# Memory transposes written ahead of the last head pair's q and k, and new tiles for the memory's low parts and two outputs

## The chip, the cores and the metric

One core of a Trainium2 chip runs the whole program, one execution at a time. The metric is the device time of one execution in microseconds. Before the change it is 1638.81 us (median of 3 runs, 1638.03 to 1639.77).

## The reference

A trunk of two layers over 512 tokens of width 1024, all in f32. Each layer has three sublayers, and each of these adds its normalised result to the running state:

```python
h = h + rms_norm(mixer(rms_norm(h, mix_pre_g[i])), mix_post_g[i])
y = memory_cross_attention(rms_norm(h, mem_pre_g[i]), rms_norm(mem, mem_kv_g[i]),
                           x_wq[i], x_wkv[i], x_wo[i])
h = h + rms_norm(y, mem_post_g[i])
h = h + rms_norm(swiglu_ffn(rms_norm(h, ffn_pre_g[i]), w_gate_up[i], w_down[i]), ffn_post_g[i])
```

The mixer of layer 0 is dilated attention: 16 heads of 64, three patterns of window and stride whose softmaxes are merged. The mixer of layer 1 is differential attention: 8 heads, each with two softmaxes, `(p1 - lam * p2) @ v`, and an RMS norm of each head's output. Cross attention has 4 heads of 256 over 256 memory tokens: the queries come from the state, keys and values from the normalised memory. What matters below is that the memory's keys and values depend on the memory and on weights alone, and so can be computed at any time before the cross attention.

## The kernel before

**Number format.** Every large product is made of three fp32r products: each operand is split into a high part (a rounded copy) and a low part (what is left), and hi*hi, hi*lo and lo*hi are added in PSUM. A split is one ScalarE copy and one VectorE subtract: L229/L230 for activations, L269/L270 for a weight page of 128x1024, L320/L321 behind a transpose.

**Storage.** R[0] to R[21] are tiles of 128x2x512, high part and low part side by side. A tile has many tenants in turn. PSUM has eight banks: banks 0 and 1 (in the mixers) collect projections, 2, 4 and 5 take attention scores, 3 takes probability times value ("pv"), 6 and 7 take transposes alternately. f0 to f3 hold softmax rows, f8 and f9 hold outputs, wh0 to wh2 and wl0 to wl2 hold split weights. A spare weight also goes into R tiles when those are free; the lists of "spares" (L1358 for the cross attention) say which tile and from which mark on.

**The mixer.** Heads are worked on in 8 pairs. `ORDER` (L895) says in which order the projections are written: `v` a quarter of the values, `k`, `q` or `p` (both) for one pair, `m` the loading and normalising of the memory's two halves into the tiles named g0 and m7 (m7 lies in R[7]). Attention of a pair is: scores (L683, L684), softmax, transposes of the probability tiles (L316), pv (L757 in layer 0; L780 to L782 in layer 1), output. In layer 1 the output of a head goes through a mean square by matmul (L791), a VectorE transpose of blocks (L793), an inverse root on GpSimd (L797), the transpose back (L798) and the scaling L802, after which PSUM bank 3 is free for the next pv. Outputs are split into R[p], pair p.

**The memory.** `mem_T` transposes the two halves, four blocks of 128x512 in all (four PE transposes, one ScalarE copy and one VectorE subtract each): high parts into R[8] and R[9], low parts into R[16] and R[17]. `x_kv(0)` then makes keys (L344 to L346) and values (L953 to L955) of the first cross head. Both stand in `early`, between the mixer and its output projection `close` (w_out, L396 to L398). The first line of `early` waited for pair 6's scores and a mark of the weights; `pair_ready` (L737) let the attention of pair 7 begin only when `mem_T` had been written.

**What sets the order.** `drive` (L182) writes two streams into each other, "dense" (projections) and "att" (attention), by their estimated cost and by conditions that a stream yields. The program so written then goes through a scheduler which orders each engine's queue by the data dependencies and the position in the program; everything of the attention stream is written at a priority 200 positions ahead. On the chip each queue runs from front to back.

**Behind the last scores.** The FFN's first weights are folded sums: SyncE loads (L1158, L1161, L1164, L1166), GpSimd DMAs which add onto the loaded data (L1159, L1162), and VectorE additions (L1175). The tile "fold0" lies where pair 7's last operands of the scores (page1 in layer 0, qz in layer 1) lay, and so its first load comes after the last score.

## Time and profile before

| | |
|---|---|
| median of 3 runs | 1638.81 us |
| the profiled execution | 1638.14 us |
| its span, first to last instruction | 1636.4 us |
| TensorE busy | 1580.5 us, 97% of the span |
| VectorE, ScalarE, GpSimd busy | 67%, 48%, 22% |
| mean granted TensorE clock | 0.993 |

The span leaves 1.74 us of the execution's own time around it. In the rows below, a bracket such as `[0.34 <-DVE r L321]` says that the engine stood idle for 0.34 us before the instruction and which instruction ended that wait. Buffer numbers are left out in the trace (r for any R tile). In the rows of the order they stand, with a running number behind an underscore (r8_75 is R[8]).

### The profile page before, as it was taken

How to read it: one execution, taken by the hardware profiler on the slowest of the kernel's cores; microseconds unless marked ns; L12 is line 12 of the kernel's file. 1: busy time of each engine (PE TensorE's matmuls, PEld its weight loads, DVE VectorE, ACT ScalarE, POOL GpSimd, SP SyncE). 2: the span in 40 equal slices, each digit the busy share in tenths (PEclk: the TensorE clock that was granted, in tenths of full speed). 3: DMA queues.
4: the chain of work that ended last, by engine and by line, in shares of the span. 5: the costliest groups of instructions: out<-in, count | busy, mean ns of one | idle time of the engine just before them, and what ended most of it. 6: DMA issues, size and time to landing. Idle time of an engine off the chain costs nothing.

```text
span 1636.4 us, 25877 instructions
## 1 busy us (share of the span) xinstructions
PE 1580.5 (97%) x10064; PEld 1427.0 (87%) x10064; DVE 1089.3 (67%) x1750; ACT 779.4 (48%) x1349; POOL 365.5 (22%) x356
## 2 busy tenths in 40 slices
PE   6999989999989999999999999889999999999998
PEld 6899878899878999988898888778988899999886
DVE  7778886754557677772378888856555667778332
ACT  5566665543535444452236565634444444445221
POOL 4634420200031111100044654221001321110000
PEclk9999999999999999999999999999999999999999
DMA  5533424343315676633424434343332167774322
GB/s 219 146 91 101 114 73 135 115 131 103 115 50 128 175 181 178 159 107 99 142 91 134 121 101 115 102 145 109 105 113 79 48 179 182 180 180 124 103 91 90
DMA packets 76763, 202.63 MB, mean 124 GB/s; under 512 B 9952, under 2 KB 10208, under 8 KB 76640
## 3 DMA queue, kind: packets, MB, share of 16 engines
q1 hardware_dynamic: 65696, 181.05, 35.7%
q0 software_dynamic: 10944, 19.93, 7.7%
q8 instruction: 79, 1.29, 0.3%
q14 instruction: 44, 0.36, 0.1%
HBM read 178.40 MB, written 2.10 MB: 110 GB/s over the span
## 4 chain that ended last, share of the span: by engine, by line
PE 69%; DVE 12%; DMA 6%; issue 5%; POOL 3%; ACT 3%; SPq 0%; DVEq 0%; POOLq 0%; ACTq 0%
PE bank L396 7%; PE bank L398 7%; PE bank L397 7%; PE bank L1212 6%; PE bank L1214 6%; PE bank L1213 6%; PE bank L344 6%; PE bank L345 6%; PE bank L346 5%; DMA fold<-in_gate_up_s 4%; PE bank L316 3%; PE bank L757 1%; DVE wl L230 1%; DVE wl L270 1%; PE bank L683 1%
## 5 line engine op out<-in xcount | busy, mean ns | idle before, releaser
L270 DVE TENSOR_TENSOR wl<-page,wh 128x1024 fp32r<-128x1024 f32 x128 | 162.6, 1272 | 178.1 <-ACT wh L269 177.5
L269 ACT ACTIVATE wh<-page 128x1024 fp32r<-128x1024 f32 x155 | 163.7, 1057 | 226.2 <-PE bank L398 88.8
L344 PE MATMUL bank<-uh,wh 128*128 128x512 f32 (+1 forms) x576 | 208.3, 363 | 0.5 <-ACT uh L320 0.5
L345 PE MATMUL bank<-ul,wh 128*128 128x512 f32 (+1 forms) x576 | 207.6, 361 | 0.0
L346 PE MATMUL bank<-uh,wl 128*128 128x512 f32 (+1 forms) x576 | 207.1, 360 | 0.0
L229 ACT ACTIVATE wh<-fold 128x1024 fp32r<-128x1024 f32 x114 | 118.5, 1055 | 130.5 <-PE bank L1213 95.9
L304 POOL TENSOR_SCALAR small<-small 128x1 f32<-128x1 f32 x76 | 24.8, 326 | 641.6 <-ACT page L297 641.1
L230 DVE TENSOR_TENSOR wl<-fold,wh 128x1024 fp32r<-128x1024 f32 x114 | 138.4, 1217 | 5.8 <-ACT wh L229 5.7
L396 PE MATMUL bank<-wh,r 128*128 128x512 f32 x336 | 130.9, 394 | 2.9 <-DVE f L802 2.1
L1212 PE MATMUL bank<-r,wh 128*128 128x256 f32 x456 | 129.1, 285 | 2.8 <-DVE f L1261 2.8
L397 PE MATMUL bank<-wl,r 128*128 128x512 f32 x336 | 131.2, 391 | 0.1
L398 PE MATMUL bank<-wh,r 128*128 128x512 f32 x336 | 130.1, 391 | 0.0
L1214 PE MATMUL bank<-uh,wl 128*128 128x256 f32 x456 | 128.8, 283 | 0.0
L1213 PE MATMUL bank<-r,wh 128*128 128x256 f32 x456 | 128.3, 283 | 0.0
L1212 PE MATMUL bank<-uh,wh 128*128 128x256 f32 x456 | 126.0, 283 | 1.9 <-DVE f L1246 1.9
L1214 PE MATMUL bank<-r,wl 128*128 128x256 f32 x456 | 126.4, 283 | 0.0
L1213 PE MATMUL bank<-ul,wh 128*128 128x256 f32 x456 | 126.2, 283 | 0.0
L316 PE MATMUL bank<-ident,f 128*128 128x128 f32 x576 | 95.9, 282 | 30.1 <-DVE f L330 23.6
L344 PEld LDWEIGHTS bank<-uh,wh 128*128 128x128 f32 x576 | 111.2, 194 | 15.8 <-ACT uh L320 0.9
L346 PEld LDWEIGHTS bank<-uh,wl 128*128 128x128 f32 x576 | 111.2, 193 | 14.6 <-issue 0.5
L345 PEld LDWEIGHTS bank<-ul,wh 128*128 128x128 f32 x576 | 111.2, 193 | 14.3 <-DVE ul L321 0.3
L1175 DVE TENSOR_TENSOR fold<-fold 128x512 f32<-128x512 f32 x76 | 52.6, 692 | 99.6 <-DMA fold<-in_gate_up_s 61.5
(227 smaller groups left out, 4473.2 us busy)
## 6 DMA issues: line engine op xcount, KB each, us to landing
fold<-in_gate_up_s SPq DMA_DIRECT2D x114, 256.0 KB, 4.5
page<-in_down SPq DMA_DIRECT2D x44, 512.0 KB, 3.5
fold<-in_gate_up_s SPq DMA_DIRECT2D x38, 512.0 KB, 5.5
fold<-in_gate_up_s POOLq DMA_DIRECT2D x76, 256.0 KB, 5.3
r<-r SPq DMA_DIRECT2D x120, 128.0 KB, 2.3
page<-in_x_wk SPq DMA_DIRECT2D x16, 512.0 KB, 3.5
page<-in_x_wv SPq DMA_DIRECT2D x16, 512.0 KB, 3.5
page<-in_x_wq SPq DMA_DIRECT2D x16, 512.0 KB, 3.5
```

Of the source, the lines that this page charges most:

```text
L230: self.nc.vector.tensor_sub(lo, src, hi.bitcast(F32))
L269: self.nc.scalar.activation(hi, raw, AF.Copy)
L270: (self.nc.gpsimd if eng else self.nc.vector).tensor_tensor(lo, raw, hi.bitcast(F32), ALU.subtract)
L344: nc.tensor.matmul(out, wh[:, k], xh(k)[:, cols], start=k == 0, stop=False)
L345: nc.tensor.matmul(out, wh[:, k], xl(k)[:, cols], start=False, stop=False)
L346: nc.tensor.matmul(out, wl[:, k], xh(k)[:, cols], start=False, stop=k == DK - 1)
L396: nc.tensor.matmul(out, ah[:, ts], hi[:, kk], start=k == 0, stop=False)
L397: nc.tensor.matmul(out, ah[:, ts], lo[:, kk], start=False, stop=False)
L398: nc.tensor.matmul(out, al[:, ts], hi[:, kk], start=False, stop=k == ktiles - 1)
L1212: nc.tensor.matmul(out, wh[:, k], xh[:, k], start=first and k == 0, stop=False, **skip)
L1213: nc.tensor.matmul(out, wh[:, k], xl[:, k], start=False, stop=False, **skip)
L1214: nc.tensor.matmul(out, wl[:, k], xh[:, k], start=False, stop= k == 3, **skip)
```

## The change

`ORDER` gets a step "t" ahead of p7: once the mark ("w", 5) stands, `mem_T` is written there, ahead of the projections of pair 7. The condition on the memory in `pair_ready` goes, and `early` keeps only the gain's load and `x_kv(0)`. `mem_T` takes the four blocks in another order (first half left, second half left, second half right, first half right), and gives R[7] back between the transposes and the split of the third. The low parts go to R[6] and R[7] instead of R[16] and R[17]; the outputs of pairs 6 and 7 go to R[16] and R[17] instead of R[6] and R[7]; the keys and values of cross head 2 go to (16, 17) instead of (6, 7); and the spare weight of the cross attention that uses (16, 17) becomes free with output 5 there instead of with the last keys and values.

```diff
-    def transposes(self, u, hi, lo):
+    def transposes(self, u, hi, lo, between=None):
...
+        if between is not None:
+            between()
         tv = tb.rearrange("p (k t) -> p k t", k=4)
+        hi, lo = (hi(), lo()) if callable(hi) else (hi, lo)
...
             and ("v", p // 2) in m
-            and (p < 7 or "mem" in m)
...
+    def o_tile(self, k):
+        return self.R[k if k < 6 else 10 + k]
...
-                self.split(o32, self.R[p][:, 0], self.R[p][:, 1])
+                self.split(o32, self.o_tile(p)[:, 0], self.o_tile(p)[:, 1])
...
+            if w == "t":
+                yield lambda: ("w", 5) in seen
+                yield from self.mem_T()
+                continue
...
-    ORDER = "v0 k1 p2 v1 p3 p4 v2 p5 m p6 v3 p7"
+    ORDER = "v0 k1 p2 v1 p3 p4 v2 p5 m p6 v3 t p7"
...
-        for b, m in enumerate(self.mem):
+        for b, j in ((0, 0), (1, 0), (1, 1), (0, 1)):
...
+            self.transposes(
+                self.mem[b][:, j * S : (j + 1) * S], hi, lo,
+                (lambda: self.restore(7)) if (b, j) == (1, 1) else None,
+            )
+            yield 0.45
...
-    MEM = ((8, 9), (16, 17))
+    MEM = ((8, 9), (6, 7))
...
-        return [self.R[i] for i in ((21, 18), (12, 13), (6, 7), (21, 18))[hd]]
+        return [self.R[i] for i in ((21, 18), (12, 13), (16, 17), (21, 18))[hd]]
...
-            ((16, 17), has("xkv", 3)),
+            ((16, 17), has("o", 5)),
...
-                yield lambda: ("s", 6) in self.mark and ("w", 5) in self.mark
-                yield from self.mem_T()
                 load(0, "mem_pre_g", i)
```

The lines of the changed kernel that are named below stand 3 to 14 lines further down: L344 becomes L347, L396 L399, L683 L686, L757 L762, L780 L785, L953 L966, L321 L324, L798 L803, L802 L807, L729 L732, L1158 L1171, L1175 L1188.

**TensorE, layer 0, the memory's transposes.** g0 is the first half of the memory, m7 the second, r18 and r19 operands of pair 7's scores, r8 and r9 high parts of the memory, f0 to f3 probability rows. Before:

```order
L316 MATMUL bank7_123<-ident_107,g0_95 128x128 x4
...
L316 MATMUL bank6_122<-ident_107,g0_95 128x128 x4
L683 MATMUL bank5_121<-r19_86,r18_85 128x512
...
L684 MATMUL bank4_120<-r20_87,page1_112 128x512
L953 MATMUL bank0_116<-wh2_91,r8_75 128x256
...
L955 MATMUL bank0_116<-wh2_91,r16_83 128x256
L316 MATMUL bank7_123<-ident_107,m7_1784 128x128 x4
L316 MATMUL bank6_122<-ident_107,m7_1784 128x128 x4
L344 MATMUL bank1_117<-r8_75,wh0_89 128x256
L316 MATMUL bank7_123<-ident_107,f3_100 128x128 x4
```

and now:

```order
L316 MATMUL bank7_123<-ident_107,g0_95 128x128 x4
...
L316 MATMUL bank6_122<-ident_107,m7_1784 128x128 x4
L686 MATMUL bank5_121<-r19_86,r18_85 128x512
...
L687 MATMUL bank4_120<-r20_87,page1_112 128x512
L966 MATMUL bank0_116<-wh2_91,r8_75 128x256
...
L968 MATMUL bank0_116<-wh2_91,r6_459 128x256
L316 MATMUL bank7_123<-ident_107,m7_1784 128x128 x4
L347 MATMUL bank1_117<-r8_75,wh0_89 128x256
L316 MATMUL bank6_122<-ident_107,g0_95 128x128 x4
...
L347 MATMUL bank1_117<-r9_76,wh0_89 128x256
L316 MATMUL bank7_123<-ident_107,f3_100 128x128 x4
L316 MATMUL bank6_122<-ident_107,f0_97 128x128
```

The first transposes keep their place behind three scores of pair 7 (the L684 just ahead of them are not shown), and so pair 7's projections stay ahead of them. The last of the four moves behind the first projection on the memory, and the first transposes of a probability row behind it (f3) now stand 14 matmuls behind the last transposes of the memory, where one stood between.

**VectorE, layer 0, around the first fold addition.** wl2 is the low part of a w_out weight, r13 and r15 transposed probabilities. Before:

```order
L321 TENSOR_TENSOR r15_82<-bank7_123,r14_81 128x4x128
L710 RECIPROCAL small_110<-small_110 128x1
L1175 TENSOR_TENSOR fold0_4147<-fold0_4147 128x512
L321 TENSOR_TENSOR r13_80<-bank6_122,r12_79 128x4x128
L270 TENSOR_TENSOR wl2_94<-page0_111,wh2_91 128x1024
L1175 TENSOR_TENSOR fold0_4147<-fold0_4147 128x512
L230 TENSOR_TENSOR ul_66<-bank0_116,ul_66 128x512
L270 TENSOR_TENSOR wl0_92<-page0_111,wh0_89 128x1024
L321 TENSOR_TENSOR r13_80<-bank7_123,r12_79 128x4x128
```

and now:

```order
L324 TENSOR_TENSOR r15_82<-bank7_123,r14_81 128x4x128
L698 TENSOR_SCALAR f2_99<-f2_99,small_110 128x512
L1188 TENSOR_TENSOR fold0_4147<-fold0_4147 128x512
L270 TENSOR_TENSOR wl2_94<-page0_111,wh2_91 128x1024
L713 RECIPROCAL small_110<-small_110 128x1
L324 TENSOR_TENSOR r13_80<-bank6_122,r12_79 128x4x128
L1188 TENSOR_TENSOR fold0_4147<-fold0_4147 128x512
L230 TENSOR_TENSOR ul_66<-bank0_116,ul_66 128x512
L270 TENSOR_TENSOR wl0_92<-page0_111,wh0_89 128x1024
L324 TENSOR_TENSOR r13_80<-bank7_123,r12_79 128x4x128
```

The split of wl2 has moved ahead of the evacuation of bank 6 into r13; both stand behind the first fold addition, before and now.

**TensorE, layer 0, where the last probability rows are transposed.** wh1, wl1, wh2 and wl2 are w_out weights, r0 to r3 outputs. Before:

```order
L398 MATMUL bank2_118<-wh1_90,r1_68 128x512
L316 MATMUL bank7_123<-ident_107,f1_98 128x128
...
L757 MATMUL bank3_119<-r14_81,r11_78 128x256
L316 MATMUL bank6_122<-ident_107,f2_99 128x128 x4
L757 MATMUL bank3_119<-r15_82,r11_78 128x256
L396 MATMUL bank1_117<-wh2_91,r2_69 128x512
L397 MATMUL bank1_117<-wl2_94,r2_69 128x512
L398 MATMUL bank1_117<-wh2_91,r2_69 128x512
```

and now:

```order
L399 MATMUL bank1_117<-wh2_91,r2_69 128x512
...
L316 MATMUL bank7_123<-ident_107,f1_98 128x128
...
L762 MATMUL bank3_119<-r15_82,r11_78 128x256
L400 MATMUL bank1_117<-wl2_94,r2_69 128x512
L401 MATMUL bank1_117<-wh2_91,r2_69 128x512
L399 MATMUL bank1_117<-wh2_91,r3_70 128x512
L400 MATMUL bank1_117<-wl2_94,r3_70 128x512
L401 MATMUL bank1_117<-wh2_91,r3_70 128x512
L316 MATMUL bank6_122<-ident_107,f2_99 128x128 x4
```

Seven w_out matmuls and one pv matmul have moved ahead of the f2 transposes, and six of them use wh2 or wl2.

**TensorE, layer 1, the first, fourth and last scores of pair 7.** Before:

```order
L316 MATMUL bank6_122<-ident_107,m7_8599 128x128 x4
L683 MATMUL bank5_121<-r19_86,r18_85 128x512
L683 MATMUL bank4_120<-r19_86,r18_85 128x512
...
L344 MATMUL bank1_117<-r8_75,wh1_90 128x256
L683 MATMUL bank5_121<-r19_86,r18_85 128x512
L684 MATMUL bank5_121<-r20_87,qz_7211 128x512
...
L954 MATMUL bank0_116<-wl1_93,r9_76 128x256
L683 MATMUL bank2_118<-r19_86,r18_85 128x512
L684 MATMUL bank2_118<-r20_87,qz_7211 128x512
L955 MATMUL bank0_116<-wh1_90,r17_84 128x256
```

and now:

```order
L316 MATMUL bank6_122<-ident_107,g0_95 128x128 x4
L348 MATMUL bank1_117<-r6_6642,wh1_90 128x256
...
L349 MATMUL bank1_117<-r8_75,wl1_93 128x256
L686 MATMUL bank5_121<-r19_86,r18_85 128x512
...
L348 MATMUL bank1_117<-r7_9023,wh2_91 128x256
L686 MATMUL bank5_121<-r19_86,r18_85 128x512
...
L401 MATMUL bank1_117<-wh2_91,r1_6493 128x512
L686 MATMUL bank2_118<-r19_86,r18_85 128x512
L687 MATMUL bank2_118<-r20_87,qz_7211 128x512
L316 MATMUL bank7_123<-ident_107,f2_99 128x128 x4
```

Eleven projections on the memory now stand ahead of the first scores, the fourth score (the second on bank 5) follows 26 matmuls behind them, and the last score (bank 2) stands behind the whole of x_kv(0) and six w_out matmuls.

**VectorE, layer 1, the end of the attention.** f9 and f8 belong to the output of pair 6, f2 to the last probability rows of pair 7. Before:

```order
L270 TENSOR_TENSOR wl1_93<-page0_6398,wh1_90 128x1024
L1175 TENSOR_TENSOR fold0_10875<-fold0_10875 128x512
L321 TENSOR_TENSOR r15_82<-bank7_123,r14_81 128x4x128
L798 STREAM_TRANSPOSE f9_106<-small_110 128x512
L1175 TENSOR_TENSOR fold0_10875<-fold0_10875 128x512
L729 SCALAR_TENSOR_TENSOR f2_99<-f2_99,small_110,f3_100 128x512
L270 TENSOR_TENSOR r20_87<-page0_6398,r19_86 128x1024
L802 SCALAR_TENSOR_TENSOR f8_105<-bank3_119,gsub_115,f9_106 128x512
```

and now:

```order
L270 TENSOR_TENSOR r20_87<-page0_6398,r19_86 128x1024
L730 TENSOR_TENSOR small_110<-small_110,lam_114 128x1
L324 TENSOR_TENSOR r15_82<-bank7_123,r14_81 128x4x128
L803 STREAM_TRANSPOSE f9_106<-small_110 128x512
L1188 TENSOR_TENSOR fold0_10875<-fold0_10875 128x512
L807 SCALAR_TENSOR_TENSOR f8_105<-bank3_119,gsub_115,f9_106 128x512
L732 SCALAR_TENSOR_TENSOR f2_99<-f2_99,small_110,f3_100 128x512
L1188 TENSOR_TENSOR fold0_10875<-fold0_10875 128x512
```

The fold addition moves behind the transpose L798 (now L803), and the scaling L802 (now L807) moves up to stand right behind it. On SyncE, at the same time, three loads of w_out now stand ahead of the first load of the fold, where one stood, and the copy of ul stands ahead of the fold's third and fourth load.

## Rows read from the trace of the kernel before

**Rows 1.** The profile's page: its first part (busy time) and the first line of its fourth (shares of the chain that ended last).

```profile
PE 1580.5 (97%) x10064; PEld 1427.0 (87%) x10064; DVE 1089.3 (67%) x1750; ACT 779.4 (48%) x1349; POOL 365.5 (22%) x356
...
PE 69%; DVE 12%; DMA 6%; issue 5%; POOL 3%; ACT 3%; SPq 0%; DVEq 0%; POOLq 0%; ACTq 0%
```

**Rows 2.** Busy time by stretch (start and end in us; PE, PEld, DVE, ACT, POOL busy us with counts; granted TensorE clock; DMA share; GB/s), around the end of each mixer.

```profile
230.00:250.00 20.00, 14.83 (x89) 12.94 (x88) 18.13 (x36) 12.97 (x25) 7.08 (x6) 0.91 0.35 103
250.00:270.00 20.00, 19.63 (x150) 18.72 (x150) 13.09 (x29) 14.28 (x26) 3.03 (x3) 1.00 0.52 145
270.00:290.00 20.00, 18.95 (x94) 15.87 (x95) 11.79 (x15) 7.44 (x11) 0.00 (x0) 1.00 0.46 135
1030.00:1050.00 20.00, 15.85 (x93) 13.85 (x92) 15.88 (x31) 12.07 (x24) 6.73 (x5) 0.83 0.37 106
1050.00:1070.00 20.00, 20.00 (x125) 17.73 (x124) 12.41 (x21) 11.33 (x21) 6.43 (x5) 1.00 0.67 199
1070.00:1090.00 20.00, 15.74 (x77) 11.91 (x75) 11.58 (x15) 4.75 (x7) 3.20 (x2) 1.00 0.31 92
```

**Rows 3.** Timeline of TensorE in layer 0 (start, duration, engine, line, operation, tiles, shape, count, idle time before it and what ended it): the memory's transposes and what follows them.

```profile
247.75 0.28 PE L954 MATMUL bank<-wl,r 128*128 128x256 f32 x1
247.87 0.28 PE L955 MATMUL bank<-wh,r 128*128 128x256 f32 x1
247.99 1.05 PE L316 MATMUL bank<-ident,m 128*128 128x128 f32 x8
249.28 0.39 PE L344 MATMUL bank<-r,wh 128*128 128x256 f32 x1 [0.23 <-ACT r L320]
250.00 0.66 PE L316 MATMUL bank<-ident,f 128*128 128x128 f32 x4 [0.34 <-DVE r L321]
```

**Rows 4.** The same view, the end of the attention in layer 0.

```profile
256.00 0.39 PE L684 MATMUL bank<-r,page 128*128 128x512 f32 x1
...
269.04 0.60 PE L757 MATMUL bank<-r,r 128*128 128x256 f32 x3
270.93 0.66 PE L316 MATMUL bank<-ident,f 128*128 128x128 f32 x4 [1.29 <-DVE r L321]
271.34 0.36 PE L757 MATMUL bank<-r,r 128*128 128x256 f32 x1
271.54 0.40 PE L396 MATMUL bank<-wh,r 128*128 128x512 f32 x1
272.06 0.50 PE L397 MATMUL bank<-wl,r 128*128 128x512 f32 x1
```

**Rows 5.** Timeline of VectorE in layer 0, the same time.

```profile
264.33 0.15 DVE L710 RECIPROCAL small<-small 128x1 f32<-128x1 f32 x1
269.58 0.69 DVE L1175 TENSOR_TENSOR fold<-fold 128x512 f32<-128x512 f32 x1 [5.10 <-DMA fold<-in_gate_up_s]
270.19 0.68 DVE L321 TENSOR_TENSOR r<-bank,r 128x512 fp32r<-128x512 f32 x1
270.79 1.21 DVE L270 TENSOR_TENSOR wl<-page,wh 128x1024 fp32r<-128x1024 f32 x1
271.93 0.68 DVE L1175 TENSOR_TENSOR fold<-fold 128x512 f32<-128x512 f32 x1
```

**Rows 6.** Timeline of TensorE in layer 1: the fourth score of pair 7, its last, and two w_out matmuls.

```profile
1044.98 0.50 PE L683 MATMUL bank<-r,r 128*128 128x512 f32 x1 [0.78 <-ACT f L723]
...
1056.61 0.39 PE L683 MATMUL bank<-r,r 128*128 128x512 f32 x1
1056.84 0.39 PE L684 MATMUL bank<-r,qz 128*128 128x512 f32 x1
...
1069.35 0.39 PE L398 MATMUL bank<-wh,r 128*128 128x512 f32 x1
1069.58 0.39 PE L396 MATMUL bank<-wh,r 128*128 128x512 f32 x1
```

**Rows 7.** The same view, the waits at the end of layer 1's attention.

```profile
1074.78 0.39 PE L780 MATMUL bank<-r,r 128*128 128x256 f32 x1 [0.45 <-DVE f L802]
...
1080.90 1.13 PE L791 MATMUL bank<-f,page 128*128 128x512 f32 x2 [0.92 <-ACT f L787]
1082.84 0.50 PE L396 MATMUL bank<-wh,r 128*128 128x512 f32 x1 [0.81 <-DVE f L793]
...
1090.04 0.47 PE L396 MATMUL bank<-wh,r 128*128 128x512 f32 x1 [2.13 <-DVE f L802]
```

**Rows 8.** Timeline of VectorE in layer 1, the same time.

```profile
1059.92 1.23 DVE L270 TENSOR_TENSOR wl<-page,wh 128x1024 fp32r<-128x1024 f32 x1
...
1069.78 0.69 DVE L1175 TENSOR_TENSOR fold<-fold 128x512 f32<-128x512 f32 x1 [1.57 <-DMA fold<-in_gate_up_s]
...
1073.98 0.74 DVE L802 SCALAR_TENSOR_TENSOR f<-bank,gsub,f 128x512 f32<-128x512 f32 x1
```

**Rows 9.** Timeline of SyncE's DMA issues in layer 1.

```profile
1057.27 0.33 SPq L1158 DMA_DIRECT2D fold<-in_gate_up_s  x1
...
1061.18 0.33 SPq L253 DMA_DIRECT2D page<-in_b_out  x1
```

**Rows 10.** Timeline of GpSimd in layer 1, the same time.

```profile
1062.06 0.95 POOL L1159 DMA_DIRECT2D fold<-in_gate_up_s  x1 [23.43 <-PE bank L791]
...
1064.77 2.93 POOL L797 TENSOR_TENSOR small<-small,mhalf 128x16 f32<-128x16 f32 x1
```

**Rows 11.** Timeline of ScalarE in the cross attention of layer 0: the fourth and fifth weights split into spare tiles.

```profile
423.73 1.06 ACT L269 ACTIVATE r<-page 128x1024 fp32r<-128x1024 f32 x1 [1.34 <-DMA page<-in_x_wo]
...
427.16 1.06 ACT L269 ACTIVATE r<-page 128x1024 fp32r<-128x1024 f32 x1 [1.28 <-DMA page<-in_x_wo]
```

More of the change, by code (lines that the diff above doesn't have):

```diff
@@ L802, in rest @@
                 nc.vector.scalar_tensor_tensor(sq, pv, self.gsub, r, ALU.mult, ALU.mult)
-                self.split(sq, self.R[p][:, 0], self.R[p][:, 1])
+                self.split(sq, self.o_tile(p)[:, 0], self.o_tile(p)[:, 1])
                 self.mark["o", p] = self.clock
@@ L910, in mem_T @@
     def mem_T(self):
-        for b, m in enumerate(self.mem):
+        for b, j in ((0, 0), (1, 0), (1, 1), (0, 1)):
             ts = slice(b * P, (b + 1) * P)
-            for j in range(2):
-                hi, lo = [
-                    self.R[self.MEM[s][j]].rearrange("p a (b t) -> p (a b) t", b=2)[:, :, ts]
-                    for s in (0, 1)
-                ]
-                self.transposes(m[:, j * S : (j + 1) * S], hi, lo)
-                yield 0.45
-        self.restore(7)
+            hi, lo = [
+                lambda i=self.MEM[s][j], ts=ts: self.R[i].rearrange(
+                    "p a (b t) -> p (a b) t", b=2
+                )[:, :, ts]
+                for s in (0, 1)
+            ]
+            self.transposes(
[3 more added lines that the diff above has]
+            yield 0.45
         self.mark["mem"] = self.clock
-    MEM = ((8, 9), (16, 17))
+    MEM = ((8, 9), (6, 7))
     def memr(self, s, k):
@@ L1327, in o_act, with x_act @@
         def o_act(k):
+            return self.o_tile(k)[:, 0], self.o_tile(k)[:, 1]
+        def x_act(k):
             return self.R[k][:, 0], self.R[k][:, 1]
@@ L1410, in emit @@
                 self.close(
-                    t["x_wo"][i], DK, o_act, o_ready, get("mem_post_g"), get("ffn_pre_g"),
+                    t["x_wo"][i], DK, x_act, o_ready, get("mem_post_g"), get("ffn_pre_g"),
                     cross_spares,
```

## The prediction, made before the result was known

> **What bounds the kernel.** I read the page first: TensorE is busy 97% of the span, and the chain that ended last lies on it for 69% [rows 1]. So an edit counts by the gaps that it closes or opens on TensorE; time won on another engine counts only where TensorE waits for it. Next the busy time by stretch, to see whether there are gaps where the change works [rows 2]. Those around the memory's transposes have 14.83 and 15.85 us of work in 20, those behind the last scores 19.63, 18.95, 20.00 and 15.74. The granted clock is 1.00 in four of the six and 0.91 and 0.83 in the others; that low clock follows waits that stand in the queue ahead of the changed place, so I count nothing for it. Last the timelines of TensorE, VectorE and SyncE in these stretches, for which wait ends last, and the order of before and now beside them.
>
> The order decides what is to be costed. On TensorE both programs are the same up to the first memory transpose, in both layers: the transposes are written earlier, but their data do not free them earlier in the scheduler's list, and pair 7's q and k stay in front of them. What moves is the third and fourth block, the scores of pair 7 in layer 1, the w_out matmuls, and VectorE's queue at the end of each attention. No work is added or removed: the same 16 memory transposes per layer, the same splits, the same DMAs.
>
> **Layer 0, the transposes.** Before, the key projections wait 0.23 us for the copy of the last memory block, and the f3 transposes 0.34 us for the subtract that empties bank 7 [rows 3]. Now the last block stands behind the first projection, r9 is asked for only after 12 projections on r8, and the f3 transposes come 14 matmuls behind the last block. A 128x256 matmul follows another in 0.12 us [rows 3], so that is 14 x 0.12 = 1.7 us of cover, against the 0.96 us that lay between the last transposes' end (249.04) and the start of f3's (250.00). Both waits go: 0.57 us, as far as the next wait lets it through.
>
> **Layer 0, the end of the attention.** That next wait is the f2 transposes: 1.29 us for L321, which empties bank 6 and itself stands behind the fold addition on VectorE [rows 4, 5]. The addition waited 5.10 us for the fold's DMAs. These start after the last score (page1 comes free), which now has 0.9 us more of matmuls in front and 0.57 us less of waits: the fold comes some 0.3 us later, so the addition runs from 269.9 to 270.5. Behind it now stands the wl2 split first (1.21 us, rows 5), ready at 271.7. And TensorE now wants wl2 earlier: six w_out matmuls with wh2 or wl2 have moved ahead of f2. It arrives there at about 269.65 (the same amount of work ahead, +0.57, and the 0.57 won), waits until 271.7, does five w_out matmuls at 0.23 us each [rows 6], and starts f2 at about 272.85, where L321 was ready at 272.4. That is 1.92 us later than 270.93, but with seven w_out and one pv matmul done that stood behind it: 7 x 0.227 + 0.12 = 1.71. The rest, +0.21, is offset by the wait for wl (271.54 to 272.06, 0.29 more than the usual step, rows 4), which goes. Sum for layer 0: -0.1. Bounds: if all waits here went, 0.57 + 1.29 + 0.29 = -2.15; if the wait for wl2 (2.05) stood in full and nothing of the rest was won but the 0.57, +1.5.
>
> At this place a rule of the Trainium skill speaks against the change. Rows 5 show L321 starting as the fold addition gets off VectorE, after 5.10 us in which it stood idle with L321's data there. The page "PSUM — Partial Sum Buffer", section "Engine vs sequencer instructions", says that the queues of ScalarE, VectorE and GpSimd are strictly first in, first out. By that rule whatever is put behind the addition waits with it, and wl2 ahead of L321 costs its 1.21 us in full; were the queue free to pass the waiting addition, L321 and the wl2 split would be done by 267 and layer 0 would gain over 1 us. The rows agree with the rule.
>
> **Layer 1, the scores.** The fourth score of pair 7 waited 0.78 us for an exponential that frees its bank [rows 6]; now 26 matmuls (3.1 us) stand between it and the first scores, and the wait goes: -0.78. In exchange the scores come later. Between the third memory block and the last score now stand 25 value projections and six w_out matmuls more, and one block of four transposes less (0.35 us): 25 x 0.12 + 6 x 0.227 - 0.35 = 4.0 us. Less 0.78, the last score moves from 1056.6 to about 1059.9.
>
> **Layer 1, the end of the attention.** The fold's load went out at 1057.27, as the last score ended [rows 6, 9], and the addition came 12.5 us later, after GpSimd's additive DMA [rows 8, 10]. Now it also stands behind a third w_out load, which waits for a page that a split frees (1061.15 before, rows 8, 9). Fold issue at about 1060.6 to 1061.2, addition at 1073.1 to 1073.7. GpSimd's root L797 stands behind the additive DMAs in its queue and slides along, from 1067.7 to 1071 at its end [rows 10]; L803 behind it is still in time ahead of the addition. What counts is L802, now L807, which frees bank 3 for the next pv: before it ended at 1074.72 [rows 8], with four other VectorE instructions between it and the addition; now it follows the addition at once: 1073.1 to 1073.7, plus 0.6 and 0.74, so 1074.4 to 1075.05. Of the work on TensorE 0.28 us more stands behind this pv now. Against 1074.78 - 0.28 the pv is at -0.05 to +0.55; I take +0.2, the middle. The 0.78 that was won is spent in this wait. The last f2 transposes and their evacuation now come some 0.5 us later, but have 2 us of w_out in front of the pv that needs them. The later waits of this tail (0.92, 0.81, 2.13, rows 7) hang on the chain of the last output and stay. Sum for layer 1: +0.2. Bounds: if the 0.78 and all four waits of rows 7 went, -5.1; if the whole tail slid with the last score, +3.3.
>
> **The tiles.** Low parts of the memory in R[6] and R[7] and outputs in R[16] and R[17] cost the same splits. R[7] is where the second memory half lay, which is why it is given back between transposes and split; that wait is for four transposes that are just ahead: nothing. In the cross attention the spare weight in (16, 17) now waits for output 5. Before, the fourth and fifth spare weights were split at 423.73 and 427.16, each behind its DMA [rows 11], and no w_out matmul waited there: first use lies some 15 us later, which covers the move. Taken at 0; if the cover were gone, one weight of 1.06 + 1.23 us (ScalarE rows 11, VectorE rows 8) per layer, +2.3 each.
>
> **Sum.** -0.1 + 0.2 + 0 = +0.1 us. The profiled execution took 1638.14 us, so 1638.2 for its like; the median of the runs lies 0.67 above it, so 1638.9.
>
> **Rivals.**
> A, faster: the tail gets shorter. w_out loads no longer start in the middle of the fold's, so the fold may land as early as before although issued later; L807 behind the first addition would end near 1071.2, and the waits of 0.45 and 0.92 [rows 7] would go (-1.37), with -2.15 in layer 0: 1638.8 - 3.5 = 1635.3. For it: the DMA share of 0.67 in that stretch [rows 2]. Against it: the addition's 12.5 us hold a load, a GpSimd issue and an additive DMA one after the other.
> B, slower: VectorE's queue stands behind a fold that is issued 3 to 4 us later. If the whole tail of layer 1 slides with the last score (+3.3) and TensorE pays the wait for wl2 in layer 0 (+1.5): 1643.6. It decides from an addition in layer 1 at 1073.2 on: from there each microsecond later is one at the end, and +3.3 stands for an addition at 1076.5, a fold that takes 15 us from an issue at 1061.2 because w_out loads run beside it. For it: in layer 0 the same steps took 13.1 us (from 256.4, the last score's end in rows 4, to 269.58 in rows 5), and nothing passed the waiting addition there. Against it: the third w_out load is no new traffic, it only goes out ahead.
> C, no effect: the transposes stay behind pair 7's q and k on TensorE, and what moves behind them cancels: 1638.8.
> D, slower: the spare weight in the cross attention comes late in both layers: +4.6, 1643.5.
>
> **Chances.** Forecast 0.55, A 0.14, B 0.13, C 0.13, D 0.05. Runs of this kernel can hardly tell less than 0.2% (3.3 us) from no change; forecast and C lie within that. So faster 0.14, within 0.2% 0.68, slower 0.18. The range: 1635.0 to 1643.2 takes in A's end and most of B; what is left out are the bound of -5.1 in layer 1 and B and D at full size. The forecast's own range is 1637.0 to 1640.6.
>
> **What would show it.** In the changed profile: no wait ahead of the key projection and the f3 transposes in layer 0; a wait of about 2 us for wl ahead of a w_out matmul near 269.6 and none of 1.29 ahead of f2; no wait of 0.78 at the fourth score in layer 1, the last score near 1059.9; the fold addition near 1073.4 with a longer idle time before it, and the pv behind it near 1074.8. Wrong would be: an addition in layer 1 at 1070 (then A) or after 1075 (then B), a new wait for a weight in the cross attention (D), or memory transposes that run ahead of pair 7's q and k on the chip.

## The result and the profile after

The changed kernel takes 1642.68 us (median of 8 runs, 1641.11 to 1647.36) beside 1637.80 us for the kernel before (median of 8). The ratio is 1.0035 with a 95% interval of 1.0024 to 1.0046, some 5.7 us (the two medians lie 4.9 us apart). Medians here and below are of all runs of a kernel; ratios and mean clocks leave out the few executions that took over 1700 us. The change is slower by more than 0.2%. The forecast was 1638.9 us and no change that can be told. The time lies inside the range of 1635.0 to 1643.2, but on the side to which I had given 0.18.

The page of the changed kernel, busy time and shares of the chain [beside rows 1]:

```profile
PE 1584.8 (96%) x10064; PEld 1430.6 (87%) x10064; DVE 1089.2 (66%) x1750; ACT 779.3 (47%) x1349; POOL 367.1 (22%) x356
...
PE 69%; DVE 12%; DMA 7%; issue 4%; ACT 3%; POOL 3%; SPq 0%; DVEq 0%; POOLq 0%; ACTq 0%
```

The same matmuls are busy for 4.3 us longer. No work was added, so some of them ran at a lower clock. The mean granted clock says the same: over the 8 runs it is 0.9896, against 0.9922 over the 29 runs of before that stand beside e1 to e4. Time multiplied by clock splits the 5.8 us between the two means (1643.45 and 1637.61): an estimate of 1626.4 against 1624.8 for the part at full clock, and 17.1 against 12.8 for what half clock took. In these runs more than two thirds of the loss is clock. The 8 runs of e8 beside their own kernel before give 3.0 of 5.7 us in the same way, about half. Half clock is counted here wherever it fell, also where it cost nothing (last section).

To find the places I read the same rows in both traces. The table gives the distance between starts on TensorE: from the f transposes behind a 4.19 us wait (before the change's first place, layer 0) to the first norm transposes behind the mixer, from there to those behind the 4.04 us wait (3.92 in e10) at the end of the cross attention, and in layer 1 from the value projection behind a 2.33 us wait to the same two points. "Again" is a second profile of the changed kernel (e8). The last line is the time at half clock within the line above it.

| us | before | after | again (e8) | fold kept in layer 1 (e9) | and spares reordered (e10) |
|---|---|---|---|---|---|
| end of mixer, layer 0 | 67.64 | 68.35 | 65.27 | 66.05 | 65.00 |
| cross attention, layer 0 | 171.20 | 172.60 | 172.32 | 172.14 | 171.54 |
| end of mixer, layer 1, and cross attention | 243.90 | 248.53 | 248.78 | 244.16 | 243.38 |
| of it at half clock | 8.4 | 16.4 | 13.3 | 10.4 | 10.2 |

The loss is in layer 1 (4.6 and 4.9 us, of which 1.2 and 2.6 lie in its cross attention) and in the cross attention of layer 0 (1.1 to 1.4). With half of its half-clock time taken off, an estimate, layer 1's stretch takes 239.7 us before, 240.3 and 242.1 in the changed kernel, 239.0 in e9 and 238.3 in e10. So its loss is 4.0 us of clock and 0.6 of the rest in one profile, 2.5 and 2.4 in the other. The stretches that are left out hold nearly the same order of instructions in all these kernels, and differ by up to 4.3 us over all the profiles of this document.

**Layer 1, TensorE.** Its timeline in the changed kernel, from the last score on [beside rows 6, 7]:

```profile
1062.31 0.40 PE L686 MATMUL bank<-r,r 128*128 128x512 f32 x1
1062.54 0.40 PE L687 MATMUL bank<-r,qz 128*128 128x512 f32 x1
...
1078.42 0.58 PE L785 MATMUL bank<-r,r 128*128 128x256 f32 x1 [2.76 <-DVE f L807]
1078.80 0.42 PE L786 MATMUL bank<-r,r 128*128 128x256 f32 x1
1079.02 0.41 PE L787 MATMUL bank<-r,r 128*128 128x256 f32 x1
...
1087.84 1.12 PE L796 MATMUL bank<-f,page 128*128 128x512 f32 x2 [0.92 <-ACT f L792]
1089.77 0.50 PE L399 MATMUL bank<-wh,r 128*128 128x512 f32 x1 [0.81 <-DVE f L798]
...
1097.07 0.47 PE L399 MATMUL bank<-wh,r 128*128 128x512 f32 x1 [2.24 <-DVE f L807]
```

Layer 1 begins 3.0 us later in this execution (1037.70 against 1034.68), so the last score stands 2.7 us later than before by its own layer's clock. The wait ahead of pair 7's pv is 2.76 us where it was 0.45. Behind it the pv matmuls follow each other in 0.21 us instead of 0.12.

**Layer 1, VectorE, SyncE and GpSimd.** The timelines of the changed kernel [beside rows 8, 9, 10]:

```profile
1074.11 0.71 DVE L803 STREAM_TRANSPOSE f<-small 128x512 f32<-128x512 f32 x1 [1.23 <-POOL small L802]
1077.01 0.69 DVE L1188 TENSOR_TENSOR fold<-fold 128x512 f32<-128x512 f32 x1 [2.19 <-DMA fold<-in_gate_up_s]
1077.62 0.74 DVE L807 SCALAR_TENSOR_TENSOR f<-bank,gsub,f 128x512 f32<-128x512 f32 x1
```

```profile
1054.20 8.50 SPq L253 DMA_DIRECT2D page<-in_b_out  x3
1062.97 0.33 SPq L1171 DMA_DIRECT2D fold<-in_gate_up_s  x1
```

```profile
1068.86 0.95 POOL L1172 DMA_DIRECT2D fold<-in_gate_up_s  x1 [27.21 <-DMA fold<-in_gate_up_s]
```

The chain is all there: the fold's load goes out as the last score ends (1062.94 and 1062.97), the addition starts 14.0 us later (12.5 before), VectorE stands idle for 2.19 us ahead of it, and L807 comes right behind. GpSimd's additive DMA, which now waits for the load, goes out 5.9 us behind it (4.8 before), and the addition starts 8.2 us behind that (7.7 before). The transpose L803 had ended at 1074.82. From there to the start of L807 at 1077.62 are 2.80 us, as long as TensorE's wait.

**The clock.** Busy time by stretch in the changed kernel (columns as in rows 2), three stretches around that wait and one behind the next:

```profile
1072.00:1078.00 6.00, 3.66 (x16) 2.65 (x15) 2.39 (x4) 0.16 (x1) 3.09 (x2) 0.98 0.80 211
1078.00:1084.00 6.00, 5.58 (x21) 5.20 (x22) 2.92 (x5) 1.23 (x2) 0.00 (x0) 0.50 0.00 0
1084.00:1090.00 6.00, 4.27 (x20) 2.89 (x20) 1.94 (x2) 1.54 (x2) 0.19 (x1) 0.95 0.07 13
...
1096.00:1102.00 6.00, 4.93 (x15) 3.93 (x16) 3.24 (x5) 2.75 (x3) 0.00 (x0) 0.72 0.53 184
```

From 1078 to 1084 the granted clock is 0.50, the lower level of 1.2 GHz, directly behind the wait. Half of 6 us and the edges make an estimate of 3.4 us lost. Before, the granted clock was 1.00 from 1050 to 1090 [rows 2].

**Layer 0.** TensorE and VectorE of the changed kernel [beside rows 4, 5]:

```profile
268.34 0.72 PE L762 MATMUL bank<-r,r 128*128 128x256 f32 x4
270.90 0.50 PE L400 MATMUL bank<-wl,r 128*128 128x512 f32 x1 [1.83 <-DVE wl L270]
...
272.18 0.97 PE L316 MATMUL bank<-ident,f 128*128 128x128 f32 x4
272.80 0.77 PE L399 MATMUL bank<-wh,r 128*128 128x512 f32 x1
```

```profile
269.02 0.69 DVE L1188 TENSOR_TENSOR fold<-fold 128x512 f32<-128x512 f32 x1 [4.83 <-DMA fold<-in_gate_up_s]
269.63 1.22 DVE L270 TENSOR_TENSOR wl<-page,wh 128x1024 fp32r<-128x1024 f32 x1
```

The wait for wl2 is there (1.83 us; 0.48 in e8, 0.87 in e9), and the 1.29 us ahead of f2, the 0.23 and the 0.34 [rows 3, 4] are gone. Here too a stretch at half clock follows (the matmuls at 272.80 take 0.77 and 0.63 us), but not in e8.

**The cross attention of layer 0,** the changed kernel's TensorE and VectorE:

```profile
435.72 0.49 PE L401 MATMUL bank<-wh,r 128*128 128x512 f32 x1 [0.45 <-DVE r L230]
```

```profile
434.10 1.23 DVE L270 TENSOR_TENSOR r<-page,r 128x1024 fp32r<-128x1024 f32 x1 [1.41 <-PE bank L1054]
435.25 1.34 DVE L230 TENSOR_TENSOR r<-bank,r 128x256 fp32r<-128x256 f32 x3
```

VectorE's split of a spare weight into (16, 17) has to wait for the last pv that reads the values of cross head 2, which now lie there. The splits of the outputs stand behind it in VectorE's queue, and a w_out matmul waits for one. Before, no w_out matmul waited there.

### The profile page after: what moved, and what is told of

The parts are those of the page before. It is cut to its first block, busy times and chain, and to the rows that moved or that the text cites. A ratio compares the mean times of both kernels' runs of the same rounds, so it can differ in the third digit from the quotient of the medians.

```text
span 1643.2 us, 25865 instructions
## 1 busy us (share of the span) xinstructions
PE 1584.8 (96%) x10064; PEld 1430.6 (87%) x10064; DVE 1089.2 (66%) x1750; ACT 779.3 (47%) x1349; POOL 367.1 (22%) x356
## 3 DMA queue, kind: packets, MB, share of 16 engines
q1 hardware_dynamic: 65696, 181.05, 35.3%
q8 instruction: 79, 1.29, 0.3%
## 4 chain that ended last, share of the span: by engine, by line
PE 69%; DVE 12%; DMA 7%; issue 4%; ACT 3%; POOL 3%; SPq 0%; DVEq 0%; POOLq 0%; ACTq 0%
PE bank L399 6%; PE bank L400 6%; PE bank L401 6%; PE bank L1225 6%; PE bank L1227 6%; PE bank L1226 6%; PE bank L347 6%; PE bank L348 6%; PE bank L349 6%; DMA fold<-in_gate_up_s 4%; PE bank L316 3%; PE bank L762 1%; DVE wl L270 1%; PE bank L686 1%; DVE wl L230 1%
## 5 line engine op out<-in xcount | busy, mean ns | idle before, releaser
L347 PE MATMUL bank<-uh,wh 128*128 128x512 f32 (+1 forms) x576 | 207.8, 362 | 0.3 <-ACT uh L323 0.3
L399 PE MATMUL bank<-wh,r 128*128 128x512 f32 x336 | 131.6, 397 | 3.1 <-DVE f L807 2.2
L400 PE MATMUL bank<-wl,r 128*128 128x512 f32 x336 | 132.0, 393 | 1.8 <-DVE wl L270 1.8
L401 PE MATMUL bank<-wh,r 128*128 128x512 f32 x336 | 130.6, 392 | 0.9 <-DVE r L230 0.9
L347 PEld LDWEIGHTS bank<-uh,wh 128*128 128x128 f32 x576 | 110.6, 193 | 15.6 <-issue 0.7
L1188 DVE TENSOR_TENSOR fold<-fold 128x512 f32<-128x512 f32 x76 | 52.6, 692 | 101.0 <-DMA fold<-in_gate_up_s 63.9
```

Source lines behind the costliest of these rows:

```text
L347: nc.tensor.matmul(out, wh[:, k], xh(k)[:, cols], start=k == 0, stop=False)
L399: nc.tensor.matmul(out, ah[:, ts], hi[:, kk], start=k == 0, stop=False)
L400: nc.tensor.matmul(out, ah[:, ts], lo[:, kk], start=False, stop=False)
L401: nc.tensor.matmul(out, al[:, ts], hi[:, kk], start=False, stop=k == ktiles - 1)
```

## The experiments

Five theories were put to the test: 1, the fold addition that the later last score makes late, with the clock's fall behind its wait; 2, the tiles and the spare weight in the cross attention; 3, late scores that starve the end of layer 1 by themselves; 4, the tiles in some other way; 5, a clock that falls whatever is taken away. Each kernel was timed beside the kernel before on the same chip: e1 to e4 on one, e5 to e8 on a second, e9 to e12 on a third.

**e1 and e2: the fold's tile kept until the mixer's end.** One ScalarE copy of 128x1 into a new tenant of the tile's place, behind the mixer, so that the fold's loads and additions come later; in the changed kernel (e1) and in the kernel before (e2).

```diff
             self.drive(dense, self.attention(i), self.RATE[i])
+            hold = self.page(1, "hold")
+            self.nc.scalar.activation(hold[:, :1], self.h[3][:, :1], AF.Copy)
```

> The changed kernel, with one tiny ScalarE copy (128x1) behind the mixer's end that keeps the fold's tile until then, so that the fold's loads and additions leave the end of the attention. Theory 1 (VectorE's queue stands behind a fold addition that the later last score makes late, and the clock falls behind the wait that this makes on TensorE): the waits of 1.83 us (L400) in layer 0 and 2.76 us (L785) in layer 1 shrink to under 0.5 us each, no half clock behind them, and the time falls by 5 to 7 us from the changed kernel, to some 1636 to 1638 where before is 1638: ratio 0.998 to 1.001. Theory 2 (the tiles and the later spare weight in the cross attention cost the time): both tail waits may go, yet the time stays within 2 us of the changed kernel, ratio above 1.002. Theory 3 (the late scores themselves starve the end of layer 1): the wait ahead of L785 stays above 1.5 us, now for the softmax or the root instead of the fold.

> The kernel before, with the same tiny copy that keeps the fold's tile. Theory 1: the waits of 1.29 us (L316, layer 0) and 0.45 us (L780, layer 1) of the kernel before go, 1 to 2 us faster, ratio 0.9985 to 0.9995; the gain is smaller than in the changed kernel by 3 us or more, since there the fold came later. Theories 2 and 3: no more than 0.5 us either way.

Measured: e1 1641.17 us, ratio 1.0030 (1.0017 to 1.0044); e2 1635.99 us, ratio 0.9992 (0.9983 to 1.0002). For e2 that is what theory 1 expects, though its interval takes in no change. In e1 the waits ahead of L400 at the fold and of L785 were gone, but the time had not followed, and theory 2 seemed to be the one left. The trace showed another reason. TensorE and VectorE of e5, which has the same edit, behind the mixer of layer 0:

```profile
305.47 0.66 PE L316 MATMUL bank<-ident,f 128*128 128x128 f32 x4 [2.70 <-DVE f L333]
```

```profile
304.07 0.69 DVE L471 TENSOR_TENSOR f<-bank,g 128x512 f32<-128x512 f32 x1 [2.00 <-ACT page L297]
304.68 1.41 DVE L333 SCALAR_TENSOR_TENSOR f<-h,small,g 128x512 f32<-128x512 f32 x2
```

The scheduler had put the multiplication of the next block (L471), which waits 2.00 us for a square on ScalarE, ahead of the norm that TensorE waits for. In e1, e4 and e5 TensorE's wait there is 2.69 to 2.75 us, in the kernel before and the changed one 1.11 and 0.99; in e4 and e5 a half clock from 306 to 309 follows. That is an estimate of 1.7 us of wait and up to 1.7 of clock. More had moved in e1 and e5: in layer 1 the last score starts 21.3 and 22.8 us behind the layer's 2.33 us wait, as before (21.9), and not as in the changed kernel (24.6). So the edit changed the order as well as the fold, and neither e1 nor e5 says what the fold alone costs. e1 is 4.4 us above e9 (below) by the ratios, and what the wait and the clock leave of that is not explained.

**e3 and e12: the spare weights in the order in which their tiles come free,** in the changed kernel, run twice.

```diff
             ((8, 9), has("xkv", 3)),
-            ((16, 17), has("o", 5)),
             ((12, 13), has("o", 3)),
+            ((16, 17), has("o", 5)),
```

> The changed kernel, with the spare weights of the cross attention listed in the order in which their tiles come free: (12, 13) from output 3 ahead of (16, 17) from output 5. Theory 2: the waits of 0.45 us at L401 (two in layer 0, one in layer 1, for a VectorE split that stands behind a weight's) go, and the time falls by 2 to 3 us from the changed kernel, ratio about 1.002. Theory 1: at most 1.4 us fall, since only the three waits go, and the tails of both mixers stay as they are, with 1.8 and 2.8 us of wait; ratio 1.003.

> The changed kernel with the reordered spare weights (as e3), on the same chip as e9 to e11, for the share of the fold alone: e10 against this one. Theory 1: e10 is 2.5 to 4 us faster than this. Theory 2: this is 1.5 to 2.5 us faster than the changed kernel, ratio 1.002 to 1.0028.

Measured: 1640.87 us, ratio 1.0026 (1.0014 to 1.0038), and 1639.79 us, ratio 1.0017 (1.0004 to 1.0030); the changed kernel had 1.0035 twice. In both traces one wait of 0.29 us at L401 is left per layer, where there were 0.45 and 0.46 in layer 0 and 0.45 in layer 1, and the cross attention of layer 0 takes 171.61 and 171.55 us instead of 172.60 and 172.32. Against the changed kernel that is 1.5 and 2.9 us by the ratios, with intervals that overlap its own; the traces give 0.7 to 1.0 us in layer 0. Theory 2 explains a part, not the whole. TensorE ahead of pair 7's pv in e12, where no half clock follows:

```profile
1075.77 0.39 PE L785 MATMUL bank<-r,r 128*128 128x256 f32 x1 [2.12 <-DVE f L807]
```

**e4: the tiles and the block order alone,** with `mem_T` in `early` again and its conditions as before.

```diff
-    ORDER = "v0 k1 p2 v1 p3 p4 v2 p5 m p6 v3 t p7"
+    ORDER = "v0 k1 p2 v1 p3 p4 v2 p5 m p6 v3 p7"
...
+            and (p < 7 or "mem" in m)
...
+                yield lambda: ("s", 6) in self.mark and ("w", 5) in self.mark
+                yield from self.mem_T()
```

> The changed kernel's tiles and block order alone: mem_T is written in early again, behind the mark of pair 6's scores, and pair 7 waits for the memory again. In its order the last score of layer 1 stands three rows behind where it stood before, not 32. Theory 1: the fold of layer 1 is not late, the wait ahead of pair 7's pv stays under 1 us, and the time is 1 to 3 us above before (the cross attention's share): ratio 1.0005 to 1.002. Theory 2: the tiles carry the cost, ratio 1.003 or more. Theory 3 expects what theory 1 does for the end of layer 1.

Measured: 1641.66 us, ratio 1.0028 (1.0017 to 1.0039). The time is nearer to theory 2 and the trace to theory 1: the end of layer 1 with its cross attention takes 244.91 us, 1.0 more than before, no wait stands ahead of pair 7's pv (one of 1.27 us ahead of the f2 transposes instead), and the addition starts at 1071.38, 35.3 us behind the layer's 2.33 us wait (35.1 before). What is left for its time are the cross attention of layer 0 and the changed order ahead of it (see e1); I did not part the two. What e4 does show is that the tiles and the block order alone do not move the last score of layer 1 (21.4 us behind the wait). That the place of `mem_T` alone moves it is not shown: in e1 it has its new place, and the last score stands as early.

**e5: both edits,** the fold kept in both layers and the spares reordered.

> The changed kernel with both edits: the fold's tile kept until the mixer's end, and the spare weights in the order in which their tiles come free. Theory 1 (the late fold behind the mixers' last scores, with the clock falls behind its waits) and theory 2 (the spare weight that blocks those behind it) together carry the cost and add up: no wait over 0.5 us ahead of L400 in layer 0, of L785 in layer 1 and of L401 in the cross attention, 5 to 7 us faster than the changed kernel, ratio 0.998 to 1.001. Theory 4 (the tiles cost something that neither edit reaches): ratio stays at 1.002 or above, although those waits are gone.

Measured: 1641.53 us, ratio 1.0025 (1.0014 to 1.0036), theory 4 by the number. It has e1's order behind layer 0, quoted above, and so decides nothing.

**e6: the late spare weight in the kernel before.**

```diff
-            ((16, 17), has("xkv", 3)),
+            ((16, 17), has("o", 5)),
```

> The kernel before with one edit alone: the spare weight in (16, 17) of the cross attention is held until output 5, as in the changed kernel. Theory 2: waits of about 0.45 us at w_out matmuls of the cross attention, for an output split that stands behind a weight split on VectorE, 0.5 to 1.2 us per layer, ratio 1.0006 to 1.0015. Theory 1: nothing that the measurement can tell, ratio 1.000, and the mixers' ends as before.

Measured: 1638.37 us, ratio 1.0012 (1.0003 to 1.0021). The number is in theory 2's range, but its trace has none of the waits: no w_out matmul waits, and the two cross attentions take 171.13 and 171.06 us, as before. The instructions of every engine stand in the order of the kernel before, and the fourth and fifth spare weights are split as early (117.4 and 120.8 us behind the mixer's end in layer 0, 117.5 and 120.9 before). So the edit made no weight late here, and whether lateness alone would cost is left open; that the tile which pv still reads costs is seen in the changed kernel's trace. Where e6's 2 us went is not shown either. They stand without any change of order, so differences of some 2 us between two kernels are no proof of a cause here, even with an interval that leaves out 1.

**e7: a wait of known size,** five multiplications by 1.0 ahead of pair 6's scaling in the kernel before.

```diff
+                if p == 6:
+                    for _ in range(5):
+                        nc.vector.tensor_scalar(r, r, 1.0, None, ALU.mult)
                 nc.vector.scalar_tensor_tensor(sq, pv, self.gsub, r, ALU.mult, ALU.mult)
```

> The kernel before with five VectorE multiplications by 1.0 (0.43 us each by the 0.49 us rows of such an instruction, which overlap) ahead of the scaling L802 of pair 6 in layer 1: a wait of known size, without any late score or fold. If a wait there costs what it lasts, the wait ahead of pair 7's pv grows from 0.45 to 2.5 us and the time by 2.1 us, ratio 1.0013, at full clock behind it. If the clock falls behind such a wait, as behind the 2.76 us of the changed kernel, the time grows by 2.1 plus 1.7 to 3.4 us, ratio 1.0023 to 1.0034, with a granted clock of a half in 3 to 7 us behind it.

Measured: 1641.90 us, ratio 1.0026 (1.0015 to 1.0038), more than the 2.1 us of the wait. Its profile, TensorE and the stretch behind:

```profile
1074.92 0.39 PE L780 MATMUL bank<-r,r 128*128 128x256 f32 x1 [2.51 <-DVE f L805]
```

```profile
1072.00:1078.00 6.00, 3.49 (x22) 2.82 (x21) 3.99 (x8) 1.12 (x2) 0.00 (x0) 1.00 0.27 87
1078.00:1084.00 6.00, 4.27 (x22) 2.95 (x21) 1.94 (x2) 1.54 (x2) 0.90 (x2) 1.00 0.14 37
1084.00:1090.00 6.00, 4.05 (x18) 3.00 (x16) 3.46 (x4) 2.01 (x2) 2.30 (x1) 1.00 0.28 87
1090.00:1096.00 6.00, 5.70 (x18) 4.59 (x19) 3.10 (x4) 2.75 (x3) 0.00 (x0) 0.72 0.66 185
```

The wait has the size that was meant, and in this execution the clock stays at 1.00 behind it; it falls only behind a later wait, at 1090. Over the 12 runs the mean granted clock is 0.9910 against 0.9923 for the kernel before beside it, an estimate of 2.2 us. The time agrees with a fall in some executions; that it falls at this place is not shown.

**e8: the changed kernel again.**

> The changed kernel once more, on the same chip as the three beside it, for a second profile of it. Theory 1: the waits of 1.8 us ahead of L400 and 2.8 us ahead of L785 come again, and behind the second a stretch at half the granted clock; ratio 1.0025 to 1.0045.

Measured: 1643.25 us, ratio 1.0035 (1.0023 to 1.0048). TensorE and the stretch in its profile:

```profile
1075.83 0.58 PE L785 MATMUL bank<-r,r 128*128 128x256 f32 x1 [3.02 <-DVE f L807]
```

```profile
1072.00:1078.00 6.00, 2.98 (x14) 2.52 (x13) 3.48 (x6) 0.63 (x1) 0.53 (x1) 0.77 0.32 60
1078.00:1084.00 6.00, 5.08 (x30) 4.43 (x30) 1.58 (x2) 2.14 (x3) 0.00 (x0) 0.94 0.00 0
```

The wait and the half clock behind it came again, the clock for a shorter stretch. The wait of 1.8 us ahead of L400 was 0.48 here.

**e9, e10 and e11: the fold kept in layer 1 alone.** This edit leaves the order up to the end of layer 1's attention as it was in the changed kernel. It moves the fold's instructions from there into the cross attention of layer 1, and a few others change places around pair 7's last pv.

```diff
             self.drive(dense, self.attention(i), self.RATE[i])
+            if i == 1:
+                hold = self.page(1, "hold")
+                self.nc.scalar.activation(hold[:, :1], self.h[3][:, :1], AF.Copy)
```

> The changed kernel with the fold's tile kept until the mixer's end in layer 1 alone. In e1, e4 and e5 the order of VectorE behind the mixer of layer 0 came out otherwise too (a multiplication of the second block, L471, ahead of the norm L333, with a wait of 2.7 us on TensorE instead of 1.0); here that order is the changed kernel's own, and only the fold has left the end of layer 1's attention. Theory 1: the wait of 2.8 to 3.0 us ahead of L785 and the half clock behind it go, 2.5 to 4 us faster than the changed kernel, ratio 1.001 to 1.0022. Theory 5 (the granted clock falls somewhere in the stretch whatever is taken away): the wait goes, the time falls by less than 1.5 us, ratio 1.0028 or more.

> The changed kernel with the fold kept in layer 1 alone and the spare weights in the order in which their tiles come free. Theories 1 and 2 together: 4 to 6 us faster than the changed kernel, ratio 0.999 to 1.001: both causes named, with what layer 0 costs left in. Theory 4 (the tiles or layer 0 cost something else): 1.0015 or more.

> The kernel before with the fold's tile kept in layer 1 alone. Theory 1: only the wait of 0.45 us ahead of pair 7's pv goes, and what the fold addition holds up behind it: 0.3 to 1.5 us faster, ratio 0.999 to 0.9998. Theory 5: nothing, ratio 1.000.

Measured: e9 (changed kernel) 1638.42 us, ratio 1.0003 (0.9988 to 1.0017); e10 (with e3's spares) 1635.52 us, ratio 0.9988 (0.9975 to 1.0000); e11 (kernel before) 1637.76 us, ratio 1.0003 (0.9990 to 1.0016). TensorE and VectorE of e9:

```profile
1074.34 0.60 PE L316 MATMUL bank<-ident,f 128*128 128x128 f32 x4
1074.70 0.36 PE L785 MATMUL bank<-r,r 128*128 128x256 f32 x1
...
1081.66 0.56 PE L399 MATMUL bank<-wh,r 128*128 128x512 f32 x1 [0.81 <-DVE f L798]
1082.03 0.63 PE L400 MATMUL bank<-wl,r 128*128 128x512 f32 x1
...
1088.79 0.47 PE L399 MATMUL bank<-wh,r 128*128 128x512 f32 x1 [0.46 <-DVE f L807]
```

```profile
1068.72 0.71 DVE L803 STREAM_TRANSPOSE f<-small 128x512 f32<-128x512 f32 x1 [2.73 <-POOL small L802]
1069.47 0.75 DVE L807 SCALAR_TENSOR_TENSOR f<-bank,gsub,f 128x512 f32<-128x512 f32 x1
```

With nothing between L803 and L807 the scaling ends more than 4 us before pair 7's pv, which does not wait at all and runs at full clock. From 1.0035 to 1.0003 is 5.2 us, more than the 2.5 to 4 that I had written. The changed kernel itself was not timed on that chip; e12 was, and e10, which differs from it by the same edit, is 4.7 us below it by the ratios (0.9988 against 1.0017). In both pairs the intervals lie apart. The same edit does nothing that can be told to the kernel before. That is theory 1: what costs in the changed kernel is the fold addition in front of L807, made late by the last score. Theory 3 falls with it, since the last score of e9 stands 24.2 us behind the layer's 2.33 us wait, nearly as late as in the changed kernel (24.6; 21.9 before). Theory 5 falls by the time, though in e9's trace the clock falls at another place (last section). e10 gives what theories 1 and 2 together expect. It is the fastest version by its ratio, and its interval touches 1.

## Why the prediction was wrong

The forecast of no change failed at two terms, and both chains had been named. The end of layer 1's attention was to cost 0.2 us, and the two profiles show 3.5 and 2.2 more up to the mixer's end. The tiles were to cost nothing, and the cross attention of layer 0 takes 1.1 to 1.4 more.

**Layer 1, the end of the attention.** The mechanism held step by step: the 0.78 us wait gone, the last score some 3 us later (2.7 against 3.3), the fold's load out with the last score's end, VectorE's queue behind the addition. The rule of the Trainium skill, "PSUM — Partial Sum Buffer", section "Engine vs sequencer instructions", that these queues are strictly first in, first out, agrees with L807 in the changed kernel and in e8, where it starts 0.61 us behind the start of the addition although VectorE had stood idle ahead of that (2.19 us in the changed kernel), and with e9, where it does not wait. The sizes were off. I let the addition start 12.5 us behind its load, at 1073.1 to 1073.7; it took 14.0, and 14.3 in e8, which rival B allowed for. (Between the addition and L802 stood five instructions before, not four; nothing hangs on it.) The pv then comes 0.6 us later by its layer's clock than before (1078.42 less 3.02, against 1074.78), and in e8 1.1 us; with the 0.28 us of work more behind it that is 0.9 and 1.4, where I took +0.2. That alone would still have been within 0.2%. The other term is the one that I set to zero in the first paragraph: "I count nothing for it", of the granted clock. That was meant for the falls that were already there; for a fall behind a new wait the sum has no term. A wait of 2.76 us is followed by 6 us at a half, an estimate of 3.4 us; in e8, 3.02 us by a shorter stretch. I had costed the wait as a shift of the path and not asked what TensorE's rate would be behind it. In the first profile this is the larger of the two terms, in e8 they are about even. Rival B's side was right, its price of 4.8 us is near the measured 5.7, but only its layer 1 part came true, and with the clock in place of a full slide; that the number is near is in part luck.

**The tiles.** "First use lies some 15 us later, which covers the move. Taken at 0." The weight was in time. What was late is VectorE: the split into (16, 17) waits for pv, and the output splits queue behind it. It is 1.1 to 1.4 us in layer 0 by the table, of which the order of e3 and e12 gives back 0.7 to 1.0. In three more profiles of the order before (e6, e7, e11) this cross attention takes 171.10 to 171.13 us. Rival D looked at the weight's arrival and so at the wrong end of the same queue. What it left out is the step from a new wait on VectorE to the splits that stand behind it in the same queue.

**Layer 0** was right in its mechanism: waits of 0.23, 0.34 and 1.29 us gone, a wait for wl2 in their place (2.05 forecast; 1.83 measured in the changed kernel, but 0.48 in e8, 0.87 in e9, 0.44 in e12 and none in e3). The sum of -0.1 us was too small a gain. Over six profiles of this order (after, e3, e8, e9, e10, e12) the stretch to the mixer's end takes 65.0 to 68.4 us, 66.0 in the mean; over four of the order before (before, e6, e7, e11) 66.5 to 68.4, 67.4 in the mean. That is a gain of 1.4 us, within the bound of -2.15. The wait came near its forecast in one profile of the six. The fold was not 0.3 us later: its first load went out at 256.10, when before the last score ended at 256.39 [rows 4], and the addition started at 269.02 against 269.58.

So the parts of the change, by the ratios: 4.7 to 5.2 us from the fold in layer 1 (e10 against e12, e9), 1.5 to 3 from the order of the spare weights (e3, e12, and e10 against e9), and what would remain is a gain of some 2 us (e10 against before). The last two are no larger than e6's 2 us, and the intervals do not set them apart from nothing. Rival A was wrong for layer 1 and near for layer 0; rival C is refuted, since the change does move the time, though not by the transposes, which kept their place.

## What to carry to other kernels

When a step moves, ask which buffers its last reader frees, and what will be issued then: here a weight load for a stage more than 200 us away came late because a score came late, and its addition stood in the queue in front of the instruction that TensorE needed. A tile that is exchanged for another brings that tile's readers into the queue of whoever writes it next. A wait of TensorE can have two prices, the wait and the clock behind it; write down both. And an edit that is meant to move one instruction can move others: e1 and e5 did, and their times answered another question than the one that was put.

## What was not expected of the hardware

A half clock ahead of another wait cost nothing. In e9 the w_out matmuls from 1081.66 on run at 0.43 us each instead of 0.23 for 3.4 us, and the wait at their end is 0.46 us where it was 2.13 [rows 7]: the two L399 rows are 7.13 us apart there, and 7.20 in the kernel before at full clock. TensorE would have waited there anyway, so this fall did not count.

The same wait did not always bring the same clock. Behind the waits of 2.76, 3.02 and 2.67 us ahead of L785 (after, e8, e3) the clock fell, behind 2.51 us at the same place in e7 and 2.12 us in e12 it did not. The end of layer 1 with its cross attention took 243.97 us in e12, as long as the kernel before's 243.90, and 248.98 in e3, whose instructions stand in the same order. 7.3 us of it were at half clock in e12 and 17.1 in e3; half of that difference is 4.9 of the 5.0 us. Why the clock falls in one execution and not in another is left open. The spread of whole runs is not in the clock alone: in e8 they reach from 1638.94 to 1645.16 us, with mean granted clocks of 0.990 and 0.989.
